# Memory heads' weighted sums with the values stationary, and the last tile's products in two halves

## The chip, the core and the metric

The kernel runs on one core of one Trainium2 chip. The metric is the device time of one execution in microseconds; for several runs the median is given. The profiled execution is one more run, with the hardware profiler's record of every instruction. In the profile PE is the tensor engine's matmul, PEld its weight load, DVE the vector engine, ACT the scalar engine, POOL the GpSimd engine and SP the engine that issues most of the transfers (DMAs).

## The reference

Two layers over 256 tokens of width 2048. Each layer projects the normed tokens to 7168 columns, runs three groups of heads on them and projects the result back:

```
h = rmsnorm(x);  proj = h @ w_in[l]              # 2048 -> 7168
y_a = short_gated_conv(a_x, a_b, a_c) * silu(a_g)
y_d = headnorm(diff_attention(q, k, v)) * silu(d_g)    # 6 heads of 128
mk, mv = keys and values of 256 memory tokens          # 4 heads of 128
p   = softmax(rmsnorm(m_q) @ mk^T / sqrt(128))
y_m = (p @ mv) * silu(m_g)                             # the memory heads
x = x + concat(y_a, y_d, y_m) @ w_out[l]
```

All of it is in float32. The changed part is `p @ mv`, its scaling by one over the softmax's sum and by the gate, and the very last tile of the last layer's output projection.

## The kernel before

Tokens lie as two tiles (t = 0, 1) of 128 rows, the width as 16 tiles k of 128. A product with a weight matrix is done by `block` (L306): 512 output columns, all k, both token tiles, with the turned tokens as the stationary side and the weights as the moving side. Float32 accuracy comes from splitting: each operand is a rounded part hi and a remainder lo, both in the type fp32r, and `products` (L298) issues three matmuls (hi hi, hi lo, lo hi). Weights come in by `load_w` (L283), two k at a time: SP loads a raw tile (L288), ACT rounds it to hi (L291), DVE subtracts to get lo (L292). There are four raw buffers and four pairs of hi and lo; a pair of buffers feeds 12 block matmuls.

Attention runs beside the blocks as generators. After each two k of a block `run_side` steps every generator that is due; a `yield n` asks to be stepped again n such steps later. Instructions marked by `keep_in_program_order` stay in the order in which they are written on their engine; the others (matmuls, weight loads) are placed by a scheduler.

Heads go in pairs, by `pair` (L501), for differential and memory heads alike. Its stages for two memory heads:

- `mem_scores` (L589): split queries and keys, six matmuls of 128x256 for each head (L604 to L606), the maximum, exp into a tile e with its sums, and r = gain / sum.
- DVE turns e in blocks of 32x32 into a sheet `sh` (L516), and `carry` (L416) brings the blocks to their places through DRAM: four DMAs out (L421), two steps later four DMAs back (L425), all on SP.
- `weighted` (L437): for each head four matmuls of 128x128 in plain float32 (L442), with the turned exp as the stationary side and the values as the moving side; the result po has queries as rows. The profile counts each plain float32 matmul as two.
- `mem_out` (L619): yn = po times r times the gate (L621), two DVE instructions for each head.
- yn is turned in blocks (L533), carried through DRAM as well, and `split_T` (L254) splits the turned result into hi and lo columns of yT, the stationary side of the output projection: ACT for hi (L258), DVE for lo (L259).

The counters `held` keep the generators from holding more than two buffers of a kind. The tiles tagged `v` and `ga` hold the differential heads' values and gate.

The output projection is four blocks of 512 columns. The products with the heads' k of the first two blocks come first, then those with the convolution's. In the last layer's last block `apart=4` puts the second token tile's products for the last four k at the very end, in `late` (L330). Then each tile's result is added to xs in halves of 256 columns (L1081), and each half is sent out (L1084), the first by SP's queue, the second by ACT's.

Of the kernel before, what the change touches and what calls it, by code (L numbers as in the profile page):

```python
# [10 lines left out]
F32 = mybir.dt.float32  # L11
F32R = mybir.dt.float32r
I32 = mybir.dt.int32
AF = mybir.ActivationFunctionType
ALU = mybir.AluOpType
# [3 lines left out]
P = 128  # L19
D_MODEL = 2048  # L20
SEQ = 256
DEPTH = 2
NT = SEQ // P
# [4 lines left out]
CG = W_CONV // P  # L28
DH = W_DIFF // P
# [3 lines left out]
NB = 512  # L33
CK = 2
PARTS = 8
B = 32
NA = P // B
PAIR_EVERY = 9
# [9 lines left out]
def encoder(ctx: ExitStack, tc: tile.TileContext, x, mem, norm_g, w_in, conv_w, conv_b,  # L48
            dq_g, dk_g, lq1, lk1, lq2, lk2, head_g, mem_norm_g, w_mem_kv, mq_g, mk_g, w_out, out):
    nc = tc.nc  # L50
# [9 lines left out]
    keep = pool("keep", 1)  # L60
    tmp = pool("tmp", 2)
    small = pool("small", 3)
    dram = pool("dram", 1, bass.MemoryType.DRAM)
    ps_acc = pool("ps_acc", 4, PSUM)
    ps_s = pool("ps_s", 2, PSUM)
    ps_t = pool("ps_t", 2, PSUM)
# [3 lines left out]
    def nm(s):  # L70
        uid[0] += 1
        return f"{s}_{uid[0]}"
# [181 lines left out]
    def split_T(dst, k, src, gain, pin=False):  # L254

        hi, lo = dst[:, 0, k, :], dst[:, 1, k, :]
        if gain is None:
            both = (nc.scalar.copy(hi, src),  # L258
                    nc.vector.tensor_tensor(lo, src, hi.bitcast(F32), ALU.subtract))  # L259
        else:  # L260
            both = (nc.scalar.activation(hi, src, AF.Copy, scale=gain),  # L261
                    nc.vector.scalar_tensor_tensor(lo, src, gain, hi.bitcast(F32), ALU.mult, ALU.subtract))
        if pin:
            for i in both:
                tc.keep_in_program_order(i)
        made.add((id(dst), k))
# [31 lines left out]
    def products(stat, acc, t, k, hi, lo, first, last, pinned=False):  # L298
        sh = stat[:, 0, k, t * P:(t + 1) * P]
        sl = stat[:, 1, k, t * P:(t + 1) * P]  # L300
        for left, right, start, stop in ((sh, hi, first, False), (sh, lo, False, False), (sl, hi, False, last)):
            i = nc.tensor.matmul(acc, left, right, start=start, stop=stop)  # L302
            if pinned:
                tc.keep_in_program_order(i)

    def block(stat, w, cols, order, steps=1, apart=0, acc=None, more=False, rows=row_tiles, ready=None):  # L306


        begun = acc is not None
        if not begun:  # L310
            acc = accumulators()
        n = len(order)

        def ends(k):
            return k == order[0] and not begun, k == order[-1] and not more

        late = []
        for c in range(0, n, CK):
            k0 = order[c]
            parts = ready(c // CK) if ready else load_w(rows(w, k0), cols)  # L320
            for j in range(CK):
                k = k0 + j
                settle(stat, k)
                for t in range(NT):
                    if t > 0 and c >= n - apart:
                        late.append((t, k, *parts[j]))
                    else:
                        products(stat, acc[t], t, k, *parts[j], *ends(k))
            run_side(steps)
        for t, k, hi, lo in late:  # L330
            products(stat, acc[t], t, k, hi, lo, *ends(k))
        return acc

    def row_stats(ss, tag):
# [81 lines left out]
    def carry(sheet, to):  # L416


        d = dram.tile([NA, B, NA, sheet.shape[-1]], F32, name=nm("d"))
        for a in range(NA):  # L420
            tc.keep_in_program_order(nc.sync.dma_start(d[:, :, a].rearrange("b c r -> c b r"), sheet[a * B:(a + 1) * B]))  # L421
        yield 2
        of = d.rearrange("b c a (n i) -> (b c) a n i", i=B)
        for a in range(NA):
            tc.keep_in_program_order(nc.sync.dma_start(to[:, :, a], of[:, a]))  # L425
# [8 lines left out]
    def strips(v):  # L434
        return v.rearrange("p (b c) -> p b c", c=B)
# [61 lines left out]
    scored = set()  # L497

    held = {"e": 0, "sh": 0, "yn": 0}

    def pair(heads, begin, end, v):  # L501

        es = []
        for h in heads:
            while held["e"] == 2:
                yield 1
            held["e"] += 1
            es.append((yield from begin(h)))
            yield 2
        yield 4  # L510
        while held["sh"] == 2:
            yield 1
        held["sh"] += 1
        sh = tmp.tile([P, NA, 2, NT * NT, B], F32, tag="sh", name=nm("sh"))
        for i, e in enumerate(es):
            tc.keep_in_program_order(nc.vector.transpose(  # L516
                sh[:, :, i], e[0].rearrange("p t (k b c) -> p b (t k) c", k=NT, b=NA)))
            held["e"] -= 1
            yield 1
        yield 4  # L520
        flat = sh.rearrange("p b h n c -> p (b h n c)")
        yield from carry(sh.rearrange("p b h n c -> p b (h n c)"), flat.rearrange("p (n a i) -> p n a i", a=NA, i=B))
        eT = flat.rearrange("p (h t k q) -> p h t k q", h=2, t=NT, k=NT)
        while held["yn"] == 2:
            yield 1
        held["yn"] += 1
        yn = tmp.tile([P, NA, 2, NT, B], F32, tag="yn", name=nm("yn"))
        for i, h in enumerate(heads):
            end[0](h, yn[:, :, i], weighted(eT, i, v, h), *es[i][1:])
            yield 2  # L530
        held["sh"] -= 1
        yield 5
        tc.keep_in_program_order(nc.vector.transpose(yn, yn))  # L533
        yield 5
        flat = yn.rearrange("p b h t c -> p (b h t c)")
        yield from carry(yn.rearrange("p b h t c -> p b (h t c)"), flat.rearrange("p (n a i) -> p n a i", a=NA, i=B))
        for i, h in enumerate(heads):
            end[1](h, flat[:, i * SEQ:(i + 1) * SEQ])
            yield 1
        held["yn"] -= 1  # L540
# [75 lines left out]
        nc.vector.tensor_tensor(r, r, st[:, HR], ALU.mult)  # L616
        return e, r

    def mem_out(h, yn, po, r, a):  # L619
        for i in range(NT):  # L620
            nc.vector.scalar_tensor_tensor(yn[:, :, i], strips(po[:, i, :]), r[:, i:i + 1],  # L621
                                           strips(a[:, i, h * P:(h + 1) * P]), ALU.mult, ALU.mult)

    def rows_T(src, k, n):

# [53 lines left out]
    def T_tile(what):  # L679
        kept.append(big.tile([P, 2, KT, SEQ], F32R, tag="T", name=nm(what)))  # L680
        return kept[-1]
# [14 lines left out]
    pin = tc.keep_in_program_order  # L696
# [48 lines left out]
    class Memory:  # L745
# [66 lines left out]
        def split(self, k, turned):  # L812
            for j, pt in enumerate(turned):
                split_T(memT, k + j, pt, None, pin=True)

    mkT, mv, stm, away = [], [], [], []
# [81 lines left out]
    while s < DEPTH * KT:  # L898
        l, k = divmod(s, KT)
# [24 lines left out]
    for l in range(DEPTH):  # L924
        st = stats_of(ssx, "st")
# [3 lines left out]


        yT = T_tile("yT")
        k2 = keep.tile([P, 2, DH - 4, SEQ], F32R, tag="bgT", name=nm("k2"))

        def x_block(cols, order=ALLK, **how):
# [2 lines left out]
        def begin_pair(n, p):  # L937
            tasks.append(later(p, max(1, start + PAIR_EVERY * n - chunk[0])))
# [4 lines left out]
        for b in order:  # L943
            if b in begun:
                acc = x_block([(C_D + b * NB, NB)], ALLK[-QT:], acc=begun[b])
            else:
                acc = x_block([(C_D + b * NB, NB)], ready=m.ready if l == 0 and b == order[0] else None)
            if b == 3:
                v = keep.tile([P, NT, W_DIFF], F32, tag="v", name=nm("v"))
                ga = keep.tile([P, NT, W_DIFF], F32, tag="ga", name=nm("ga"))  # L950
            if b == 4:
                start = chunk[0]
# [20 lines left out]
        acc = x_block([(C_M, NB)])  # L973
# [7 lines left out]
        acc = x_block([(C_M + W_MEM, NB)])  # L981
        for t in range(NT):
            silu2(mga[:, t, :], acc[t], st, t)
        def mem_done(h, y):
            assert all((l, d) in scored for d in range(DH))
            split_T(yT, CG + DH + h, y, None, pin=True)

        for n in range(MH // 2):
            begin_pair(DH // 2 + n, pair((2 * n, 2 * n + 1), lambda h: mem_scores(l, h, st),
                                         (lambda h, yn, po, r: mem_out(h, yn, po, r, mga), mem_done), mv[l]))  # L990


        bg = sheet(keep, "bgx", CG)
# [79 lines left out]
        for b in range(4):  # L1073
            final = l + 1 == DEPTH
            acc = block(yT, w_out[l], [(b * NB, NB)], convs if b < 2 else heads + convs,
                        apart=4 if final and b == 3 else 0, acc=accs[b] if b < 2 else None)
            for t in range(NT):
                n = 256 if final else NB
                for lo in range(0, NB, n):
                    xc = xs[:, t, b * NB + lo:b * NB + lo + n]  # L1080
                    nc.vector.tensor_tensor(xc, acc[t][:, lo:lo + n], xc, ALU.add)  # L1081
                    if final:
                        eng = nc.scalar if lo else nc.sync
                        eng.dma_start(out[t * P:(t + 1) * P, b * NB + lo:b * NB + lo + n], xc)  # L1084
                if not final:
                    x_square(b, t)
            if l + 1 < DEPTH:
                tasks.append(later(x_next(xT, l + 1, b), 5))
# [31 lines left out]
```

## Time and profile before

| | |
|---|---|
| median of 3 runs | 924.28 us (923.7 to 924.42) |
| profiled execution | 923.66 us, of it span 921.9 us |
| TensorE matmuls busy | 916.2 us, 99% of the span |
| VectorE, ScalarE busy | 670.0 us (73%), 498.2 us (54%) |
| TensorE clock | 1.0 of full speed over the span |
| traffic | 215.13 MB, mean 233 GB/s |

The span is the time from the first to the last record of the execution. Groups are sets of instructions of one line, engine, operation and tile: the numbers behind the bar are their busy time, the mean duration of one in ns, the idle time of the engine before them and what ended it. A matmul's record covers its way through the array, and records of successive matmuls overlap; the distance from start to start is what one costs in a stream. The chain that ended last is followed back from the last instruction, and tells on which engine the end depends.

### The profile page before, as it was taken

Reading aid. Unit: us, or ns where it says so; the run is one execution under the profiler, and the core shown is the slowest. Engines: PE = TensorE matmul, PEld = TensorE weight load, DVE = VectorE, ACT = ScalarE, POOL = GpSimd, SP = SyncE. Lnnn points to the kernel's source line nnn. Section 1 sums busy time; section 2 is a strip of 40 time slices with the busy share of each in tenths; the row PEclk is TensorE's granted clock in tenths of the full one; section 3 lists DMA queues with packets and bytes.
Section 4 is the critical chain, followed back from the end, with each engine's and each line's share of the span. In section 5 each row is a group of like instructions: output and inputs, shape, how many; then the busy total and the mean of one; then the engine's idle time right before and its main releaser. Section 6 shows DMA issues by size and latency. Waiting matters only on the chain.

```text
span 921.9 us, 12335 instructions
## 1 busy us (share of the span) xinstructions
PE 916.2 (99%) x4184; PEld 760.6 (83%) x4184; DVE 670.0 (73%) x1192; ACT 498.2 (54%) x765; POOL 36.7 (4%) x66
## 2 busy tenths in 40 slices
PE   9999999999999999999999999999999999999998
PEld 6888888888888888888888888888888888888886
DVE  5579978857798696467676757878898777458652
ACT  5667645675545554445555554568554554446431
POOL 2334010000000000000000000000000000000000
PEclk9999999999999999999999999999999999999999
DMA  8889877976669988999687766885889897979662
GB/s 289 289 244 267 272 240 223 268 212 196 182 215 246 245 246 247 229 283 259 216 265 233 246 190 219 239 231 181 242 230 227 250 232 219 265 239 256 209 221 73
DMA packets 247024, 215.13 MB, mean 233 GB/s; under 512 B 132130, under 2 KB 172912, under 8 KB 246960
## 3 DMA queue, kind: packets, MB, share of 16 engines
q1 hardware_dynamic: 242080, 208.71, 77.5%
q0 software_dynamic: 3680, 4.56, 2.1%
q10 hardware_dynamic: 1200, 1.07, 0.4%
q8 instruction: 33, 0.54, 0.2%
q14 instruction: 31, 0.25, 0.1%
HBM read 193.26 MB, written 20.97 MB: 232 GB/s over the span
## 4 chain that ended last, share of the span: by engine, by line
PE 99%; ACT 0%; DVE 0%; issue 0%; DVEq 0%
PE acc L302 94%; PE po L442 2%; PE s L550 1%; PE s L549 1%; PE pt L629 0%; PE acc L799 0%; PE s L606 0%; PE s L604 0%; PE s L605 0%; PE warm L123 0%; ACT hi L781 0%; DVE lo L782 0%; DVE xs L1081 0%; ACT memT L258 0%; DVEq L1115 0%
## 5 line engine op out<-in xcount | busy, mean ns | idle before, releaser
L302 PE MATMUL acc<-hi,xT 128*128 128x512 f32 x1792 | 559.6, 390 | 0.0
L292 DVE TENSOR_TENSOR lo<-raw,hi 128x1024 fp32r<-128x1024 f32 x280 | 342.0, 1223 | 182.5 <-ACT hi L291 176.5
L291 ACT CAST hi<-raw 128x1024 fp32r<-128x1024 f32 x280 | 294.4, 1052 | 333.1 <-PE acc L302 268.9
L302 PEld LDWEIGHTS acc<-hi,xT 128*128 128x128 f32 x1792 | 336.4, 188 | 69.0
L302 PE MATMUL acc<-lo,xT 128*128 128x512 f32 x896 | 349.0, 389 | 0.0
L302 PEld LDWEIGHTS acc<-lo,xT 128*128 128x128 f32 x896 | 168.3, 188 | 33.6
L302 PE MATMUL acc<-hi,yT 128*128 128x512 f32 x512 | 157.9, 389 | 0.0
L302 PEld LDWEIGHTS acc<-hi,yT 128*128 128x128 f32 x512 | 96.1, 188 | 19.9
L302 PE MATMUL acc<-lo,yT 128*128 128x512 f32 x256 | 99.6, 389 | 0.0
L302 PE MATMUL acc<-hi,memT 128*128 128x512 f32 x248 | 78.4, 393 | 0.0
L302 PEld LDWEIGHTS acc<-lo,yT 128*128 128x128 f32 x256 | 48.0, 188 | 10.0
L302 PEld LDWEIGHTS acc<-hi,memT 128*128 128x128 f32 x248 | 46.0, 188 | 9.5
L782 DVE SCALAR_TENSOR_TENSOR lo<-raw,cva,hi 128x1024 fp32r<-128x1024 f32 (+1 forms) x34 | 41.0, 1219 | 15.0 <-ACT hi L781 14.8
L302 PE MATMUL acc<-lo,memT 128*128 128x512 f32 x124 | 48.0, 391 | 0.3 <-DVE lo L782 0.3
L781 ACT ACTIVATE hi<-raw,cva 128x1024 fp32r<-128x1024 f32 (+1 forms) x34 | 36.6, 1099 | 10.7 <-DMA raw<-in_w_mem_kv_dram 6.4
L302 PEld LDWEIGHTS acc<-lo,memT 128*128 128x128 f32 x124 | 23.3, 188 | 5.7 <-DVE lo L782 0.9
L560 ACT ACTIVATE e<-e,mx 128x256 f32<-128x256 f32 x48 | 23.8, 499 | 1.4 <-DVE mx L556 1.3
L646 POOL DMA_DIRECT2D xt<-in_x_dram x32 | 21.5, 680 | 18.8 <-DVE rsy L186 14.2
L404 DVE STREAM_TRANSPOSE sh<-sh 128x1024 f32<-128x1024 f32 (+2 forms) x14 | 17.3, 1238 | 0.0
L554 DVE SCALAR_TENSOR_TENSOR e<-dist,s 128x512 f32<-128x512 f32 x24 | 15.7, 680 | 2.2 <-PE s L550 1.7
L261 ACT ACTIVATE xT<-xf,gx 128x256 fp32r<-128x256 f32 x32 | 14.4, 501 | 4.7 <-DVE xf L652 4.0
L1081 DVE TENSOR_TENSOR xs<-acc,xs 128x256 f32<-128x256 f32 (+1 forms) x24 | 10.9, 505 | 7.8 <-PE acc L302 7.8
(168 smaller groups left out, 598.8 us busy)
## 6 DMA issues: line engine op xcount, KB each, us to landing
raw<-in_w_in_dram SPq DMA_DIRECT2D x192, 512.0 KB, 4.3
raw<-in_w_out_dram SPq DMA_DIRECT2D x64, 512.0 KB, 4.3
raw<-in_w_in_dram SPq DMA_DIRECT2D x64, 256.0 KB, 4.4
raw<-in_w_mem_kv_dram SPq DMA_DIRECT2D x30, 512.0 KB, 6.0
d<-sh SPq DMA_DIRECT2D x80, 128.0 KB, 3.8
sh<-d SPq DMA_DIRECT2D x64, 128.0 KB, 4.0
d<-yn SPq DMA_DIRECT2D x40, 64.0 KB, 4.1
yn<-d SPq DMA_DIRECT2D x40, 64.0 KB, 3.3
```

The lines of the kernel that those rows point to most:

```text
L261: both = (nc.scalar.activation(hi, src, AF.Copy, scale=gain), nc.vector.scalar_tensor_tensor(lo, src, gain, hi.bitcast(F32), ALU.mult, ALU ...
L291: nc.scalar.copy(hi, raw)
L292: nc.vector.tensor_tensor(lo_, raw, hi.bitcast(F32), ALU.subtract)
L302: i = nc.tensor.matmul(acc, left, right, start=start, stop=stop)
L404: tc.keep_in_program_order(nc.vector.transpose(src, src))
L442: nc.tensor.matmul(po[:, t, :], eT[:, i, t, k, :], v[:, k, h * P:(h + 1) * P], start=k == 0, stop=k == NT - 1)
L554: nc.vector.scalar_tensor_tensor(e[:, c], dist, -slopes[h], s[c], ALU.mult, ALU.add)
L560: nc.scalar.activation(e[:, c, i], e[:, c, i], AF.Exp, bias=mx[:, c, i:i + 1], accum_out=sm[:, c, i:i + 1])
L646: tc.keep_in_program_order(nc.gpsimd.dma_start(st[:, n], src[n * B:(n + 1) * B].rearrange("p (b r) -> b p r", b=NA)))
L781: both = (nc.scalar.activation(hi[:, j], raw[:, j], AF.Copy, scale=g), nc.vector.scalar_tensor_tensor(lo[:, j], raw[:, j], g, hi[:, j].bit ...
L782: nc.vector.scalar_tensor_tensor(lo[:, j], raw[:, j], g, hi[:, j].bitcast(F32), ALU.mult, ALU.subtract))
L1081: nc.vector.tensor_tensor(xc, acc[t][:, lo:lo + n], xc, ALU.add)
```

## The change

For memory heads `pair`, `weighted` and `mem_out` are replaced by one generator, `mem_pair`. The stationary side of the weighted sum is now the values and the moving side the turned exp, over all 256 queries at once; both are split into hi and lo in fp32r, three matmuls for each of two tiles of memory tokens, so six of 128x256 for each head. The result has head columns as rows and queries as columns, as yT wants it, so it isn't turned any more. Instead the gate, scaled by r, is turned and carried through DRAM ahead of the sum, right behind the exp sheet, and DVE multiplies po by it. The split parts lie in tiles with the tags `v` and `ga`.

In the last block the last three of the four products set apart are issued first for columns 0 to 255, into the accumulator, and then for columns 256 to 511, into a new PSUM tile of their own. The second half is then added to xs in two steps: what the accumulator has of it, and the new tile.

```
+SPLIT = 3
...
-        for t, k, hi, lo in late:
+        whole = late[:-SPLIT] if apart else late
+        for t, k, hi, lo in whole:
             products(stat, acc[t], t, k, hi, lo, *ends(k))
+        if apart:
+            near, far = slice(0, NB // 2), slice(NB // 2, NB)
+            for t, k, hi, lo in late[-SPLIT:]:
+                products(stat, acc[t][:, near], t, k, hi[:, near], lo[:, near], *ends(k))
+            acc.append(ps_acc.tile([P, NB // 2], F32, tag="acc", name=nm("rest")))
+            for i, (t, k, hi, lo) in enumerate(late[-SPLIT:]):
+                products(stat, acc[-1], t, k, hi[:, far], lo[:, far], i == 0, i == SPLIT - 1)
         return acc
...
-    def mem_out(h, yn, po, r, a):
...
+    def mem_pair(l, n, a, st):
...
+        for i, (e, r) in enumerate(es):
+            tc.keep_in_program_order(nc.vector.transpose(
+                sh[:, :, i], e.rearrange("p t (k b c) -> p b (t k) c", k=NT, b=NA)))
+            held["e"] -= 1
+            for t in range(NT):
+                nc.vector.tensor_scalar(yn[:, :, i, t], strips(a[:, t, heads[i] * P:(heads[i] + 1) * P]),
+                                        r[:, t:t + 1], None, ALU.mult)
+            yield 1
+        tc.keep_in_program_order(nc.vector.transpose(yn, yn))
+        yield 4
+        eT = sh.rearrange("p b h n c -> p (b h n c)")
+        yT_ = yn.rearrange("p b h t c -> p (b h t c)")
+        yield from carry(sh...)
+        yield from carry(yn...)
+        if n == 0:
+            spare[l] = [keep.tile([P, 3, NB], F32R, tag=tag, name=nm(tag)) for tag in ("v", "ga")]
+        hi, lo = spare[l]
...
+        yield 1
+        for k in range(NT):
+            c = slice(k * SEQ, (k + 1) * SEQ)
+            src = mv[l][:, k, n * SEQ:(n + 1) * SEQ]
+            tc.keep_in_program_order(nc.scalar.copy(hi[:, 0, c], src))
+            tc.keep_in_program_order(nc.vector.tensor_tensor(lo[:, 0, c], src, hi[:, 0, c].bitcast(F32), ALU.subtract))
+        split(1, eT[:, 0:NB])
+        yield 1
+        split(2, eT[:, NB:2 * NB])
+        held["sh"] -= 1
+        yield 1
+        for i, h in enumerate(heads):
+            po = ps_t.tile([P, SEQ], F32, tag="t", name=nm("po"))
+            at = 0
+            for k in range(NT):
+                vh, vl = (t[:, 0, k * SEQ + i * P:k * SEQ + (i + 1) * P] for t in (hi, lo))
+                eh, el = (t[:, 1 + i].rearrange("p (t k q) -> p t k q", t=NT, k=NT)[:, :, k] for t in (hi, lo))
+                for left, right in ((vh, eh), (vh, el), (vl, eh)):
+                    nc.tensor.matmul(po, left, right, start=at == 0, stop=at == 3 * NT - 1)
+                    at += 1
+            y = yT_[:, i * SEQ:(i + 1) * SEQ]
+            nc.vector.tensor_tensor(y, po, y, ALU.mult)
+            yield 2
+            assert all((l, d) in scored for d in range(DH))
+            split_T(yTs[l], CG + DH + h, y, None, pin=True)
+        held["yn"] -= 1
...
-            begin_pair(DH // 2 + n, pair((2 * n, 2 * n + 1), lambda h: mem_scores(l, h, st),
-                                         (lambda h, yn, po, r: mem_out(h, yn, po, r, mga), mem_done), mv[l]))
+            begin_pair(DH // 2 + n, mem_pair(l, n, mga, st))
...
                     nc.vector.tensor_tensor(xc, acc[t][:, lo:lo + n], xc, ALU.add)
+                    if t == NT - 1 and lo > 0 and len(acc) > NT:
+                        nc.vector.tensor_tensor(xc, acc[NT], xc, ALU.add)
```

More of the change, by code (lines that the diff above doesn't have):

```diff
@@ L617, in mem_scores, with split @@
         return e, r
-    def mem_out(h, yn, po, r, a):
-        for i in range(NT):
-            nc.vector.scalar_tensor_tensor(yn[:, :, i], strips(po[:, i, :]), r[:, i:i + 1],
-                                           strips(a[:, i, h * P:(h + 1) * P]), ALU.mult, ALU.mult)
+    spare, yTs = {}, {}
+    def mem_pair(l, n, a, st):
+        heads = (2 * n, 2 * n + 1)
+        es = []
+        for h in heads:
+            while held["e"] == 2:
+                yield 1
+            held["e"] += 1
+            es.append((yield from mem_scores(l, h, st)))
+            yield 2
+        yield 4
+        while held["sh"] == 2 or held["yn"] == 2:
+            yield 1
+        held["sh"] += 1
+        held["yn"] += 1
+        sh = tmp.tile([P, NA, 2, NT * NT, B], F32, tag="sh", name=nm("sh"))
+        yn = tmp.tile([P, NA, 2, NT, B], F32, tag="yn", name=nm("yn"))
+        for i, (e, r) in enumerate(es):
[7 more added lines that the diff above has]
+        tc.keep_in_program_order(nc.vector.transpose(yn, yn))
+        yield 4
+        eT = sh.rearrange("p b h n c -> p (b h n c)")
+        yT_ = yn.rearrange("p b h t c -> p (b h t c)")
+        yield from carry(sh.rearrange("p b h n c -> p b (h n c)"), eT.rearrange("p (n a i) -> p n a i", a=NA, i=B))
+        yield from carry(yn.rearrange("p b h t c -> p b (h t c)"), yT_.rearrange("p (n a i) -> p n a i", a=NA, i=B))
+        if n == 0:
+            spare[l] = [keep.tile([P, 3, NB], F32R, tag=tag, name=nm(tag)) for tag in ("v", "ga")]
+        hi, lo = spare[l]
+        def split(j, src):
+            tc.keep_in_program_order(nc.scalar.copy(hi[:, j], src))
+            tc.keep_in_program_order(nc.vector.tensor_tensor(lo[:, j], src, hi[:, j].bitcast(F32), ALU.subtract))
+        yield 1
[5 more added lines that the diff above has]
+        split(1, eT[:, 0:NB])
+        yield 1
+        split(2, eT[:, NB:2 * NB])
+        held["sh"] -= 1
+        yield 1
+        for i, h in enumerate(heads):
[9 more added lines that the diff above has]
+            nc.vector.tensor_tensor(y, po, y, ALU.mult)
+            yield 2
+            assert all((l, d) in scored for d in range(DH))
+            split_T(yTs[l], CG + DH + h, y, None, pin=True)
+        held["yn"] -= 1
@@ L931, in encoder @@
         yT = T_tile("yT")
+        yTs[l] = yT
         k2 = keep.tile([P, 2, DH - 4, SEQ], F32R, tag="bgT", name=nm("k2"))
@@ L983, in encoder @@
             silu2(mga[:, t, :], acc[t], st, t)
-        def mem_done(h, y):
-            assert all((l, d) in scored for d in range(DH))
-            split_T(yT, CG + DH + h, y, None, pin=True)
         for n in range(MH // 2):
-            begin_pair(DH // 2 + n, pair((2 * n, 2 * n + 1), lambda h: mem_scores(l, h, st),
-                                         (lambda h, yn, po, r: mem_out(h, yn, po, r, mga), mem_done), mv[l]))
+            begin_pair(DH // 2 + n, mem_pair(l, n, mga, st))
         bg = sheet(keep, "bgx", CG)
```

## The prediction

> **What bounds the kernel now.** I read the page's first and fourth parts (busy time and the chain that ended last), then who waited for whom, then TensorE's instructions in order of time round one memory head and at the end.
>
> ```profile
> span 921.9 us, 12335 instructions
> PE 916.2 (99%) x4184; PEld 760.6 (83%) x4184; DVE 670.0 (73%) x1192; ACT 498.2 (54%) x765; POOL 36.7 (4%) x66
> ...
> PE 99%; ACT 0%; DVE 0%; issue 0%; DVEq 0%
> PE acc L302 94%; PE po L442 2%; PE s L550 1%; PE s L549 1%; PE pt L629 0%; PE acc L799 0%; PE s L606 0%; PE s L604 0%; PE s L605 0%; PE warm L123 0%; ACT hi L781 0%; DVE lo L782 0%; DVE xs L1081 0%; ACT memT L258 0%; DVEq L1115 0%
> ```
>
> The chain is TensorE for 99%, so a matmul that becomes shorter shortens the span by as much, as long as its operands lie ready. Whether they do is told by the waits (who, for whom, us in total, times, longest) and by three groups, the matmuls with an idle time of 0.0 and the two that make the weight parts:
>
> ```profile
> ACT hi L291 <- PE acc L302: 268.9, 176, 3.0
> DVE lo L292 <- ACT hi L291: 176.5, 175, 4.9
> ...
> ACT hi L291 <- DMA raw<-in_w_in_dram: 24.7, 12, 5.1
> ```
>
> ```profile
> L302 PE MATMUL acc<-hi,xT 128*128 128x512 f32 x1792 | 559.6, 390 | 0.0
> L292 DVE TENSOR_TENSOR lo<-raw,hi 128x1024 fp32r<-128x1024 f32 x280 | 342.0, 1223 | 182.5 <-ACT hi L291 176.5
> L291 ACT CAST hi<-raw 128x1024 fp32r<-128x1024 f32 x280 | 294.4, 1052 | 333.1 <-PE acc L302 268.9
> ```
>
> ScalarE, which rounds the weights to hi, mostly waits for TensorE to free a buffer: the weights are ahead by all four buffer pairs. Each pair feeds 12 matmuls. When TensorE frees one, 3 pairs (36 matmuls) are still ahead, and its refill takes 1.05 + 1.22 = 2.3 us.
>
> **The change on TensorE.** First the rows of one old memory head (start, duration, instruction), then of one scores step of a memory head, which issues six fp32r matmuls of 256 columns each with its own weight load, as the new weighted sum does.
>
> ```profile
> 793.25 0.40 PE L302 MATMUL acc<-hi,xT 128*128 128x512 f32 x1
> 793.48 1.06 PE L442 MATMUL po<-mv,sh 128*128 128x128 f32 x8
> 794.29 0.47 PE L302 MATMUL acc<-hi,xT 128*128 128x512 f32 x1
> 794.61 0.39 PE L302 MATMUL acc<-lo,xT 128*128 128x512 f32 x1
> ```
>
> ```profile
> 752.30 0.39 PE L302 MATMUL acc<-lo,xT 128*128 128x512 f32 x1
> 752.53 0.40 PE L302 MATMUL acc<-hi,xT 128*128 128x512 f32 x1
> 752.76 0.28 PE L604 MATMUL s<-parts 128*128 128x256 f32 x1
> 752.88 0.28 PE L605 MATMUL s<-parts 128*128 128x256 f32 x1
> ...
> 753.36 0.28 PE L606 MATMUL s<-parts 128*128 128x256 f32 x1
> 753.48 0.39 PE L302 MATMUL acc<-hi,xT 128*128 128x512 f32 x1
> 753.71 0.40 PE L302 MATMUL acc<-lo,xT 128*128 128x512 f32 x1
> ```
>
> A block matmul takes 0.227 us from start to start (752.30 to 752.53). From the last one before the head to the second one after it are 794.61 - 793.25 = 1.36 us; without the head it would be 2 x 0.227 = 0.454. So an old head costs **0.906 us**: eight fp32 passes at about 0.112 and a slow restart. The same bracket round the scores is 753.71 - 752.53 = 1.18, less 0.454: six matmuls cost **0.726 us**, 0.120 each. Eight heads in two layers: 8 x (0.906 - 0.726) = **1.44 us less**. The new moving operand is read in two runs of 128, a form that no row shows; it is bounded by 0.12 (the scores) and by the weight load's duration, 0.19 (a rival below). I take 0.12, the row with the same columns, type and loads.
>
> **The end.** The last products and what follows them:
>
> ```profile
> 917.54 0.39 PE L302 MATMUL acc<-hi,yT 128*128 128x512 f32 x1
> 917.96 0.76 DVE L1081 TENSOR_TENSOR xs<-acc,xs 128x256 f32<-128x256 f32 x2 [1.96 <-PE acc L302]
> 918.42 0.33 SPq L1084 DMA_DIRECT2D out_dram<-xs  x1
> 918.75 0.34 ACTq L1084 DMA_DIRECT2D out_dram<-xs  x1
> ```
>
> Nine 512-column matmuls become 18 of 256. First start to last end was 8 x 0.227 + 0.39 = 2.21 us and becomes 17 x 0.12 + 0.28 = 2.32: 0.11 more. From the last matmul's end (917.93) to the last issue (918.75) are 0.82 us with two adds. Now the near half's add and its DMA, and the first add of the far half, run beside the nine far matmuls (9 x 0.12 = 1.08 us against 0.76 for two adds); one add of about 0.42 is left, with the same 0.03 on either side: 0.48, 0.34 less. If that cover were gone, the third add would cost the 0.34 back. The DMA left over is as large as before and goes alone. Together **0.23 us less**.
>
> **Work put beside TensorE.** Rows for the new instructions and their room:
>
> ```profile
> L621 DVE SCALAR_TENSOR_TENSOR yn<-po,mr,mga 128x128 f32<-128x128 f32 x16 | 4.8, 340 | 0.8 <-PE po L442 0.8
> L475 DVE TENSOR_TENSOR yT<-sh,yT 64x512 fp32r<-64x512 f32 x4 | 2.7, 686 | 0.1
> L259 DVE TENSOR_TENSOR yT<-yn,yT 128x256 fp32r<-128x256 f32 x8 | 3.3, 410 | 0.0
> L474 ACT CAST yT<-sh 64x512 fp32r<-64x512 f32 x4 | 2.5, 617 | 0.0
> L258 ACT CAST yT<-yn 128x256 fp32r<-128x256 f32 x8 | 3.2, 402 | 0.1
> ```
>
> ```profile
> 350.00:370.00 20.00, 20.00 (x97) 16.78 (x97) 15.47 (x20) 8.84 (x11) 0.00 (x0) 1.00 0.79 247
> 370.00:390.00 20.00, 20.00 (x94) 16.68 (x93) 8.50 (x9) 8.16 (x9) 0.00 (x0) 1.00 1.07 239
> ...
> 760.00:780.00 20.00, 20.00 (x98) 16.78 (x97) 15.47 (x20) 8.64 (x11) 0.00 (x0) 1.00 0.76 227
> 780.00:800.00 20.00, 20.00 (x95) 16.67 (x94) 9.55 (x10) 8.62 (x9) 0.00 (x0) 1.00 1.11 247
> ```
>
> (Columns of the second: PE, PEld, DVE, ACT and POOL busy in each 20 us, clock, DMA share, GB/s.) For each pair of heads DVE gets two subtractions of 128x512 (0.69 each), two of 128x256 for the values and two products with po (0.41 each): 1.37 + 0.82 + 0.82 = 3.0 us. The four scalings by gate (0.34 at most) only replace L621's four, and the transposes stay as many. ACT gets 2 x 0.62 + 2 x 0.40 = 2.0 us. In the order of the changed program the splits come one or two weight pairs after the gated sheet's long transpose (L404), at about 366 and 778 us; the second pair of each layer falls into 390 to 410 and 800 to 820. DVE then has 18.5 busy of 20 us in the fullest stretch: it may fall behind for a moment, by 1 to 2 us, and lives on the lead over TensorE: 36 x 0.227 = 8.2 us less the 2.3, some 5.9 us (an estimate from the rows above). So these cost nothing; what would cost is a lead of zero.
>
> **The queues.** Sheet and gate are carried through DRAM before the sum, in one go on SP:
>
> ```profile
> raw<-in_w_in_dram SPq DMA_DIRECT2D x192, 512.0 KB, 4.3
> ...
> d<-sh SPq DMA_DIRECT2D x80, 128.0 KB, 3.8
> sh<-d SPq DMA_DIRECT2D x64, 128.0 KB, 4.0
> d<-yn SPq DMA_DIRECT2D x40, 64.0 KB, 4.1
> yn<-d SPq DMA_DIRECT2D x40, 64.0 KB, 3.3
> ```
>
> The number and sizes of these transfers do not change; the sheet's and the gate's ways now follow each other. Where the way back is issued one weight pair (12 x 0.227 = 2.7 us) behind the way out, SP stands for 4.1 - 2.7 = 1.4 us, with the weight loads behind it. Those are issued when a raw buffer frees, four pairs (10.9 us) before ACT needs them, and take 4.3: 6.6 us of slack, and the 5.9 behind it. POOL's queue has nothing here. VectorE's product waits for po, then for the gate's way back, with the next weights' lo behind it; the gate's DMAs are issued over 10 us earlier. The old yn was turned and carried after po, with two five-step pauses; that goes, so yT's last four columns come earlier relative to po. The second pair's scores move 36 matmuls later, on TensorE at the same cost. The buffers of v and ga that hold the parts were last read for the differential heads, some 100 matmuls before; the end's third accumulator takes a PSUM buffer that the block before has long left.
>
> **Sum.** 1.44 + 0.23 = 1.67 us. The profiled run took 923.66 with a span of 921.9, 1.76 outside it; its span would be 920.2 and it 922.0. It lies 0.62 under the median of 924.28, against which I forecast **922.6 us** (0.18% less). A measurement of this kernel can tell about 0.2%, 1.85 us, from no change; the forecast lies just inside.
>
> **Rivals.**
> *The saving is handed back* (weights, not TensorE, set the pace, so the change brings less than it says): only the 0.23 is left, 924.05. For it: 12 waits for raw weights, 24.7 us. Against: 268.9 us of waiting for TensorE. Chance 0.05.
> *The lead runs out* (slower): in the first pair of each layer SP stands with its two returns and raw weights come late while DVE is at 18.5 of 20. It decides once SP stands 12.5 us (6.6 + 5.9); each us beyond is one lost. With 2 us lost in each layer: 922.6 + 4 = 926.6. For it: the longest wait for raw weights, 5.1. Against: even that is under half of 12.5. Chance 0.07.
> *The load is not hidden* (slower): if a 256-column matmul costs its weight load, 0.19, a head costs 6 x 0.19 = 1.14, 0.23 more than the old: +1.9; the end 18 x 0.19 - 9 x 0.227 - 0.34 = +1.0: 927.2. Against: the scores' 0.12 with loads. Chance 0.03. [...]
> *Shorter still*: a step of 0.227 / 2 = 0.113 without the scores' overhead: 48 x 0.007 + 18 x 0.007 = 0.46 more, 922.1. Chance 0.05. [...]
>
> **How the numbers follow.** The forecast's case has 0.80. Its own spread, 0.4 us by the shown runs (923.7 to 924.42), puts near half of it past the 0.2% bound: 0.39 of the 0.80. With *shorter still*, faster is 0.44; same is 0.41 + 0.05 = 0.46; slower 0.10. The range, 921.8 to 924.2, takes in *shorter still* and *handed back* with the runs' spread, and leaves out the slower cases and some tails.
>
> **What would show it.** Right: po's group reads 48 fp32r matmuls of 128x256, a block matmul follows each six at 0.12, one add stands behind the last matmul, and TensorE has no new idle. Wrong: an idle of L302 behind lo or raw between 340 and 420 or 750 and 840 us; po 0.19 apart; two adds after the last product.

## The result and the profile after

| | before | after |
|---|---|---|
| median of 6 runs each | 923.77 us (923.28 to 924.42) | 927.02 us (925.93 to 928.07) |
| profiled execution, of it span | 923.66, 921.9 us | 926.78, 925.0 us |

The changed kernel takes 1.0034 of the time of the one before (95% interval 1.0024 to 1.0044): 3.25 us slower where 1.67 us less was forecast, and outside the range of 921.8 to 924.2.

The page of the changed kernel: the first part, the chain of work that ended last by engine and by line, and the group of block matmuls.

```profile
span 925.0 us, 12351 instructions
PE 917.3 (99%) x4177; PEld 761.3 (82%) x4177; DVE 680.4 (74%) x1217; ACT 505.7 (55%) x781; POOL 36.6 (4%) x66
...
PE 94%; SPq 3%; DMA 1%; DVE 1%; issue 0%; ACT 0%; ACTq 0%; DVEq 0%
PE acc L303 89%; DMA raw<-in_w_in_dram 1%; SPq L434 1%; PE po L451 1%; SPq L430 1%; PE s L559 1%; PE s L558 1%; DVE lo L293 0%; PE acc L870 0%; PE po L686 0%; PE pt L700 0%; SPq L289 0%; PE warm L124 0%; ACT hi L292 0%; PE s L615 0%
...
L303 PE MATMUL acc<-hi,xT 128*128 128x512 f32 x1792 | 560.0, 391 | 1.9 <-ACT hi L292 1.9
```

TensorE's busy share still reads 99%, but the chain is no longer TensorE alone: SP's issues of the carries (L430 out, L434 back) and the landing of raw weights are on it. The matmul group, which had no idle time, has 1.9 us behind hi. Whom ScalarE waits for, when it makes hi, has moved from TensorE to the raw weights (us in total, times, longest):

```profile
ACT hi L292 <- PE acc L303: 230.5, 156, 3.0
...
ACT hi L292 <- DMA raw<-in_w_in_dram: 56.4, 31, 7.0
```

Before, the waits for raw weights were 24.7 us, 12 times, at most 5.1. The place is seen in TensorE's instructions in order of time, and in the busy times round it (PE, PEld, DVE, ACT, POOL, then the clock, the DMA share and GB/s):

```profile
394.05 0.39 PE L303 MATMUL acc<-hi,xT 128*128 128x512 f32 x1
396.37 0.50 PE L303 MATMUL acc<-hi,xT 128*128 128x512 f32 x1 [1.93 <-ACT hi L292]
397.63 0.56 PE L303 MATMUL acc<-lo,xT 128*128 128x512 f32 x1 [0.76 <-DVE lo L293]
397.99 1.05 PE L303 MATMUL acc<-hi,xT 128*128 128x512 f32 x2
398.84 0.63 PE L303 MATMUL acc<-lo,xT 128*128 128x512 f32 x1
399.27 1.05 PE L303 MATMUL acc<-hi,xT 128*128 128x512 f32 x2
400.12 0.63 PE L303 MATMUL acc<-lo,xT 128*128 128x512 f32 x1
400.55 1.00 PE L303 MATMUL acc<-hi,xT 128*128 128x512 f32 x2
401.38 0.39 PE L303 MATMUL acc<-lo,xT 128*128 128x512 f32 x1
```

```profile
396.50:402.00 5.50, 4.74 (x13) 3.52 (x14) 4.80 (x6) 4.06 (x6) 0.00 (x0) 0.69 1.04 253
402.00:408.00 6.00, 6.00 (x28) 4.95 (x28) 5.29 (x6) 3.37 (x5) 0.00 (x0) 1.00 1.05 358
```

From the start at 394.05 to the one at 401.38 are 11 steps in 7.33 us, where 11 x 0.227 = 2.50 would do: 4.83 us lost. Two pauses make 3.12 of it: 396.37 - 394.05 - 0.227 = 2.09 for hi, and 397.63 - 396.37 - 0.227 = 1.03 for the lo that is subtracted after it. The other 1.7 us are a slower clock: after the pauses three matmuls take 400.12 - 398.84 = 1.28 us, 0.427 each, and the granted clock is 0.69 over 5.5 us; in the 6 us behind it is 1.00 again. The trace's clock records put it at 0.50 for 3.41 us from 397.94 on.

Why were the weights late? SP's instructions in order of time, first of the kernel before and then of the changed one. Each row is a group of DMAs issued one behind the other; L288 and L289 are the raw weights; most of these loads bring the weights of a whole pair of k, but the last two at 384.19 and the last four at 390.85 are halves of a pair's weights.

```profile
367.44 3.57 SPq L425 DMA_DIRECT2D sh<-d  x4
371.11 1.26 SPq L288 DMA_DIRECT2D raw<-in_w_in_dram  x2
372.46 6.81 SPq L425 DMA_DIRECT2D bgT<-d  x4
379.38 1.75 SPq L288 DMA_DIRECT2D raw<-in_w_in_dram  x2
381.17 2.92 SPq L421 DMA_DIRECT2D d<-yn  x4
384.19 1.43 SPq L288 DMA_DIRECT2D raw<-in_w_in_dram  x3
```

```profile
345.58 0.39 SPq L289 DMA_DIRECT2D raw<-in_w_in_dram  x1
346.08 2.14 SPq L434 DMA_DIRECT2D yn<-d  x4
348.38 3.44 SPq L434 DMA_DIRECT2D sh<-d  x4
351.87 3.82 SPq L430 DMA_DIRECT2D d<-yn  x4
355.78 1.43 SPq L289 DMA_DIRECT2D raw<-in_w_in_dram  x3
...
373.12 2.42 SPq L430 DMA_DIRECT2D d<-sh  x4
375.65 5.25 SPq L434 DMA_DIRECT2D bgT<-d  x4
381.00 2.70 SPq L289 DMA_DIRECT2D raw<-in_w_in_dram  x2
383.79 4.67 SPq L434 DMA_DIRECT2D sh<-d  x4
388.51 2.25 SPq L430 DMA_DIRECT2D d<-yn  x4
390.85 2.46 SPq L289 DMA_DIRECT2D raw<-in_w_in_dram  x5
```

A group of four carries holds SP for 2 to 7 us in the issuing instructions themselves, and the loads behind it in the queue go out only after it. Before, loads stand between every two of the groups shown: seven from 371.11 to 385.62. In the changed kernel the sheet's way back and the gate's way out are neighbours (348.38 and 351.87 for the first pair of heads, 383.79 and 388.51 for the second). Twice that shows: from 345.97 to 355.78 SP issues 12 carries and no weights (9.8 us), and from 373.12 to 390.85, 17.7 us, it issues two loads, while TensorE uses up one per 2.72. The lead (from the end of a pair's lo to its first matmul, worked out from the records) is 5.6 us for the last pair loaded before the first of these; for the next, used at 363 us, it is 0.9, recovers to 5.5 at 386, and is below zero at 396: the pair that TensorE waits for was loaded by the issue at 390.85. Its raw buffer had been free since 378.15, when the lo that read it ended, so the load went out 12.7 us later (5.6 for the same pair in the kernel before); it landed 4.3 us after its issue, where 4.4 is the median, so the transfer itself was not slow. In the kernel before the lead is nowhere under 2.2 us once the first pairs are through (up to 110 us it is as low as 1.3 in both kernels), and it is 4.7 for that pair.

### The profile page after: what moved, and what is told of

Read it like the earlier page. It is cut to its first block, busy times and chain, and to the rows that moved or that the text cites. A ratio compares the mean times of both kernels' runs of the same rounds, so it can differ in the third digit from the quotient of the medians.

```text
span 925.0 us, 12351 instructions
## 1 busy us (share of the span) xinstructions
PE 917.3 (99%) x4177; PEld 761.3 (82%) x4177; DVE 680.4 (74%) x1217; ACT 505.7 (55%) x781; POOL 36.6 (4%) x66
## 2 busy tenths in 40 slices
DMA packets 247023, 215.11 MB, mean 233 GB/s; under 512 B 132130, under 2 KB 172912, under 8 KB 246960
## 4 chain that ended last, share of the span: by engine, by line
PE 94%; SPq 3%; DMA 1%; DVE 1%; issue 0%; ACT 0%; ACTq 0%; DVEq 0%
PE acc L303 89%; DMA raw<-in_w_in_dram 1%; SPq L434 1%; PE po L451 1%; SPq L430 1%; PE s L559 1%; PE s L558 1%; DVE lo L293 0%; PE acc L870 0%; PE po L686 0%; PE pt L700 0%; SPq L289 0%; PE warm L124 0%; ACT hi L292 0%; PE s L615 0%
## 5 line engine op out<-in xcount | busy, mean ns | idle before, releaser
L303 PE MATMUL acc<-lo,yT 128*128 128x512 f32 (+1 forms) x256 | 99.3, 388 | 0.0
L262 ACT ACTIVATE xT<-xf,gx 128x256 fp32r<-128x256 f32 x32 | 14.4, 501 | 4.8 <-DVE xf L723 4.0
L723 DVE STREAM_TRANSPOSE xf<-xt 128x1024 f32<-128x1024 f32 x8 | 16.1, 2012 | 0.0
```

The source lines that it names most:

```text
L723: tc.keep_in_program_order(nc.vector.transpose(whole.rearrange("p j (n i) -> p j n i", i=B), st.rearrange("p n (c j) -> p j n c", j=QT)))
```

## The experiments

Theory Q: SP's queue. The carries that were moved together keep SP from issuing weights. Rival V: VectorE's and ScalarE's added work makes hi and lo late. Rival T: the added or moved transfers slow the weights on the DMA engines. Ratios are to the kernel before, run on the same chip, with the 95% interval.

### One part at a time

The end alone, put into the kernel before:

```
+SPLIT = 3
-        for t, k, hi, lo in late:
+        whole = late[:-SPLIT] if apart else late
...
```

> Only the last tile's end is changed; the memory heads are as before. Queue theory (the change loses time because the carries of sheet and gate stand ahead of weight loads in SP's queue in layer 0): nothing of that is here, so 0.2 us less than before (0.34 saved on the adds, 0.11 to 0.12 paid on TensorE), no idle of TensorE after the start. If the end itself were a loss (weight loads not hidden at 256 columns): about 1 us more than before.

Measured: 924.13 us, 0.9997 (0.9988 to 1.0005), which can't tell 0.23 us from nothing. The trace can: from the last matmul's end to the end of the span were 921.9 - 917.93 = 3.97 us, and in the changed kernel they are 925.0 - 921.42 = 3.58; in this run 3.60. The rows of the changed kernel:

```profile
920.38 0.76 DVE L1148 TENSOR_TENSOR xs<-acc,xs 128x256 f32<-128x256 f32 x2 [1.00 <-PE acc L303]
921.14 0.28 PE L303 MATMUL rest<-hi,yT 128*128 128x256 f32 x1
921.46 0.42 DVE L1150 TENSOR_TENSOR xs<-rest,xs 128x256 f32<-128x256 f32 x1 [0.32 <-PE rest L303]
```

Two adds end beside the far matmuls, one of 0.42 is left.

The sums alone, the changed kernel with the old end:

```
-        whole = late[:-SPLIT] if apart else late
-        for t, k, hi, lo in whole:
+        for t, k, hi, lo in late:
...
```

> Only the memory heads are changed; the end is as before. Queue theory: some 3.4 us slower than before, as TensorE waits for weight parts near 396 us in layer 0 and then runs some 2 us at a lower granted clock, against 1.4 us saved on the sums. If the end were the loss: 1.4 us faster than before.

Measured: 928.18 us, 1.0042 (1.0024 to 1.006). The loss belongs to the sums. In the profiled run TensorE pauses at 396.4 (1.02 and 0.76 us idle) and, shorter, at 813 and 819, with no fall of the clock (1.0 over the span).

The new sums in layer 1 only (with the new end):

```
-            begin_pair(DH // 2 + n, mem_pair(l, n, mga, st))
+            begin_pair(DH // 2 + n, mem_pair(l, n, mga, st) if l == 1 else
+                       pair((2 * n, 2 * n + 1), lambda h: mem_scores(l, h, st),
+                            (lambda h, yn, po, r: mem_out(h, yn, po, r, mga), mem_done), mv[l]))
```

> The new sums in layer 1 alone, the old ones in layer 0, the new end. Queue theory with the loss in layer 0: 0.7 us saved on four heads and 0.2 at the end, 0.9 us faster than before. In the trace of the changed kernel layer 1's weight parts came as late as TensorE wanted them (a lead of zero at one place), and two other traces show waits of 1 to 2 us there: if these are the rule, as slow as before or 1 us slower.

Measured: 923.69 us, 0.9997 (0.9989 to 1.0006). The pause near 396 is gone, two of 0.34 and 0.35 us idle (0.5 each from start to start) stand at 810 and 816. So layer 0's stretch makes most of the loss. The expected gain of 0.9 us (a ratio of 0.9990) lies at the edge of the interval and is not shown; in the profiled run the two pauses cost 1.0 us, about as much.

### The queue

Both carries of the memory pairs from POOL's queue, all else as changed:

```
-    def carry(sheet, to):
+    def carry(sheet, to, queue=nc.sync):
...
-        yield from carry(sh...)
-        yield from carry(yn...)
+        yield from carry(sh..., nc.gpsimd)
+        yield from carry(yn..., nc.gpsimd)
```

> The changed kernel with the memory heads' carries issued from POOL's queue in place of SP's: same transfers, same bytes, same VectorE work. Queue theory: weight loads go out on time, no idle of TensorE after the start, 1.4 to 1.7 us faster than before (922.1 where before is 923.8). VectorE theory (3.0 us more per pair make lo late): still slower than before by 2 to 3 us. Transfer theory (the DMA engines are full, whoever issues): still slower by 2 to 3 us, weight loads take longer to land.

Measured: 922.65 us, 0.9984 (0.9976 to 0.9993), 1.65 us under the 924.3 beside it, about the sum that was forecast. The busy times of one stretch, of this run and then of the changed kernel:

```profile
340.00:404.00 64.00, 64.00 (x295) 53.38 (x294) 45.21 (x64) 33.44 (x48) 21.77 (x32) 1.00 1.00 279
```

```profile
340.00:404.00 64.00, 61.31 (x273) 50.34 (x273) 40.71 (x60) 30.58 (x46) 0.00 (x0) 0.97 0.96 244
```

TensorE is busy for all 64 us although VectorE and ScalarE did more in them, against V. The waits for raw weights fall to 29.4 us. The loads issued between 340 and 402 us even take longer to land than in the changed kernel (median 5.8 and at most 10.9 us, there 4.7 and 5.7), and TensorE doesn't wait: they go out early enough, which speaks against T. But POOL's queue moves the same bytes in fewer packets (219,887 for the whole kernel against 247,023), so a part could be T.

Only the gate's carry from POOL's queue (the second of the two lines), and in a later run only the sheet's (the first):

> The changed kernel with only the gate's carry (8 of 16 DMAs a pair) issued from POOL; the exp sheet's stays in SP's queue, next to bgT's as before. Queue theory: SP issues 8 transfers less between weight loads, about 4 to 6 us of its time a pair; TensorE waits little or not, 922.2 to 923.2 where before is 923.8 to 924.3. If it took the whole of the carries to fill SP: still 1 us or more slower than before.

> The changed kernel with the sheet's two ways on POOL's queue and the gate's on SP, the counterpart of the run that moved the gate alone (still 0.18% slower). Theory (SP's issue time; the sheet's transfers with the beta and gate ones beside them are what empties the lead): no pause of TensorE near 390 to 400 us, about as with both on POOL, 922.2 to 923.4. Rival (either carry left on SP is enough): a pause of 1 to 3 us stays, 925 to 927.

Measured: the gate alone 926.11 us, 1.0018 (1.001 to 1.0027); the sheet alone 924.97 us, 1.0012 (1.0002 to 1.0021). Both times the theory's expectation missed: each carry that stays on SP is enough for a pause. With the gate moved away it is 0.82 and 0.76 us idle at 391, and from 373.48 to 391.53 SP still issues twelve carries with two loads among them. With the sheet moved away 0.71 us idle are left at 390, in a profiled run (923.43 us) that was the fastest of ten. In these two runs Q is not the whole account. The loads that came late went out 7.2 and 6.6 us after their buffers had come free, but they also took 7.7 and 7.5 us to land, 3 us over the median. Why is open, so T may have a part here.

The same transfers on SP, but three steps between the sheet's carry and the gate's:

```
         yield from carry(sh...)
+        yield 3
         yield from carry(yn...)
```

> The changed kernel with three more steps between the exp sheet's way back and the gate's way out, all still in SP's queue: as many transfers, as much VectorE work, other neighbours in the queue. Queue theory: weight loads go out between the groups, the wait near 396 us goes or falls below 1 us, 922.2 to 923.5. If the amount of transfers or VectorE's work is the cause: as slow as the changed kernel, 3 us over before.

Measured: 923.13 us, 0.9987 (0.9978 to 0.9996). Packets, bytes and the work of VectorE are those of the changed kernel; only the order in SP's queue differs. The rows of SP to compare with the changed kernel's:

```profile
382.08 6.91 SPq L434 DMA_DIRECT2D sh<-d  x4
389.09 2.60 SPq L289 DMA_DIRECT2D raw<-in_w_in_dram  x5
391.74 1.98 SPq L430 DMA_DIRECT2D d<-yn  x4
```

Five loads (one whole and four halves) go out at 389.09, ahead of the gate's way out, where the changed kernel has them at 390.85 behind it. Of the 3.1 us of pauses 0.18 is left. The margin is that thin: the lead of the same pair is -0.35 here, -1.20 in the changed kernel.

### The dose, without the change

The kernel before, with one more carry (eight DMAs of 64 KB, the gate into an unused tile) for each pair of memory heads on SP; nothing is added on TensorE, ScalarE or VectorE:

```
...
+        if more is not None:
+            extra = tmp.tile([P, NB], F32, tag="eT", name=nm("extra"), bufs=1)
+            yield from carry(more..., extra...)
...
```

> The kernel before, untouched but for one more carry on SP for each pair of memory heads: four DMAs of 64 KB out and four back, of the gate into a tile that nothing reads, right behind the exp sheet's way back. No instruction more on VectorE, ScalarE or TensorE; the old sums stand two steps later. Queue theory: weight loads come late in layer 0 where these stand beside bgT's carry, TensorE waits, 1 to 5 us slower than before. VectorE theory: as before, within 0.5 us.

And the same extra carry from POOL's queue (`carry(more..., extra..., nc.gpsimd)`):

> The dose of the run before it (one more carry of eight 64 KB transfers per pair of memory heads, put into the old kernel, 0.59% slower on SP's queue) is issued from POOL's queue; the bytes stay, the issue time leaves SP. Theory (SP's issue time between two weight loads): no idle time of TensorE at 390 to 398 us, the kernel within 0.1% of the kernel before, 923.5 to 925. Rival (the extra traffic itself, half a megabyte each way per pair, delays the weights): the pause at 393 us stays, 927 or more.

Measured: on SP 930.26 us, 1.0059 (1.0046 to 1.0072); on POOL 924.96 us, 1.0007 (0.9998 to 1.0017). The dose on SP makes the whole picture in the old kernel, pause and slow clock (granted 0.79 from 390 to 398 us, 1.00 in the 6 us after):

```profile
392.89 0.50 PE L302 MATMUL acc<-hi,xT 128*128 128x512 f32 x1 [2.63 <-ACT hi L291]
394.15 0.77 PE L302 MATMUL acc<-lo,xT 128*128 128x512 f32 x1 [0.76 <-DVE lo L292]
...
395.57 0.63 PE L302 MATMUL acc<-lo,xT 128*128 128x512 f32 x1
```

On SP the load that TensorE waits for went out 14.4 us after its buffer had come free and landed 4.6 us later. The same bytes (256 KB each way for a pair; the second expectation's half a megabyte is twice too much) from another queue leave TensorE without a pause there. V is excluded as a necessary cause, T too as far as bytes go; the packets were not held constant (10,752 more than before on SP, 1,024 on POOL). The other queue was worth 5.3 us here (930.26 - 924.96), the packets' unknown part included.

### Moves that cost elsewhere

The split's subtractions of sheet and values on POOL instead of VectorE:

```
-            tc.keep_in_program_order(nc.vector.tensor_tensor(lo[:, j], src, ...))
+            tc.keep_in_program_order(nc.gpsimd.tensor_tensor(lo[:, j], src, ...))
```

> The changed kernel with the four subtractions for lo of sheet and values done on POOL in place of VectorE: 2.2 us less for VectorE per pair, SP's queue written in the same way. Queue theory: still slower than before by 2.5 to 3.5 us, the same wait near 396 us. VectorE theory: 1.4 to 1.7 us faster than before.

Measured: 930.0 us, 1.0066 (1.0053 to 1.0079). From 360 to 404 us VectorE is busy for 24.16 us, in the changed kernel for 27.76, and the pauses stay and are more (0.67 and 0.76 at 390, 1.60 and 0.76 at 398; the wait for raw weights is 63.1 us in all). The late loads went out 9.4 and 12.0 us after their buffers had come free. V falls; why they became more was not followed up.

Both carries from ScalarE's queue (`nc.scalar` in place of `nc.gpsimd`), where they have the same packets as on SP (247,023 in all):

> The changed kernel with the memory heads' carries issued from ACT's queue: the same hardware transfers in the same small packets as on SP (on POOL's queue they went in fewer, larger packets), only out of the way of the weight loads. Queue theory: SP issues the weight loads without groups between them, no wait for raw weights beyond those of the kernel before; what ScalarE's own standing for the issues costs hi (16 issues of 0.4 to 1 us a pair) comes out of the lead, 922.3 to 924. Packet theory (the many packets of 128 bytes hold up the weight loads wherever they are issued): weight loads still late near 396 us, 926 to 927.

Measured: 932.87 us, 1.0099 (1.0083 to 1.0116). The wait for raw weights falls to 28.2 us, as Q says. But now ScalarE, which makes hi, is the one that stands: from 805.80 to 813.46 it issues DMAs, and hi stands behind them.

```profile
805.80 4.88 ACTq L434 DMA_DIRECT2D sh<-d  x3
810.72 2.74 ACTq L430 DMA_DIRECT2D d<-yn  x4
813.58 1.99 ACT L292 CAST hi<-raw 128x1024 fp32r<-128x1024 f32 x2 [7.39 <-DMA d<-yn]
```

TensorE is idle for 3.44 us up to 814.7, and in the same way for 1.44 us up to 397.6. The expected time was missed: the expectation counted ScalarE's issues (0.4 to 1 us each) and let the lead pay for them, but seven in a row took 7.7 us here, more than the lead of 5.9, with hi behind them.

The weight loads from POOL's queue, the carries on SP:

```
-            nc.sync.dma_start(raw[:, :, at:at + n], rows[:, :, lo:lo + n])
+            nc.gpsimd.dma_start(raw[:, :, at:at + n], rows[:, :, lo:lo + n])
```

> The changed kernel with the weight loads of all projection blocks issued from POOL's queue, and all carries left on SP as they are: the small packets of the carries stay. Queue theory: no weight load stands behind a carry, TensorE does not wait near 396 us; 1.4 to 1.7 us faster than before, about 922.5, unless POOL's own loads at about 90 us come late. Packet theory (the carries' packets of 128 bytes hold up the weights' transfers): TensorE still waits 2 us or more between 380 and 402 us, 926 to 927.

Measured: 932.44 us, 1.0083 (1.0066 to 1.01), far from the 922.5 expected; the profiled run took 937.42. In the disputed stretch Q holds: TensorE is busy for all of it, with the small-packet carries still on SP.

```profile
340.00:404.00 64.00, 64.00 (x295) 53.40 (x294) 49.00 (x92) 33.87 (x53) 17.85 (x26) 1.00 0.90 248
```

The time goes elsewhere, to the differential heads, whose sums wait for a sheet:

```profile
262.92 1.55 PE L451 MATMUL po<-v,sh 128*128 128x128 f32 x8 [3.00 <-DMA sh<-d]
330.74 2.05 PE L451 MATMUL po<-v,sh 128*128 128x128 f32 x8 [5.59 <-DMA sh<-d]
```

A sheet's way back lands 6.3 us after its issue here (median), 4.3 in the changed kernel. Why it lands later was not settled.

## Why the prediction was wrong

- **The queues: the step that failed.** It priced SP's standing by the wait for a landing, 4.1 - 2.7 = 1.4 us, and the issuing itself at nothing. But the rows of the carries before hold SP for 0.5 to 1.7 us per DMA, and in the changed kernel the three groups from 346.08 on, one behind the other, held SP for 9.6 us by issuing. The wait that was priced did not grow: SP waited for the landings of these ways out for 19.2 us in the whole run before and for 17.6 after. The sentence that the number and sizes of the transfers do not change was true and beside the point: what changed is how many of them lie between two weight loads. The diff and the order of the changed program show that; SP's rows of before (groups of four at 2 to 7 us) have the price. The prediction neither counts nor shows them.
- **The slack.** 5.9 us of lead is right for the steady state (5.6 worked out), and 6.6 of landing slack was taken on top of it as if all of it were free in every stretch. One standing of 9.8 us already took 4.7 us of lead; what emptied it was a second and third standing, 7.9 and 7.2 us with two loads between, before the lead had been filled again. One long standing alone did no harm: before, SP issues 16 carries and no weights from 701.33 to 710.71, 9.4 us, and TensorE doesn't wait.
- **The rival.** *The lead runs out* named the mechanism and nearly the time: 926.6 against 927.02. Its place was one pair off: the first pair's carries only took the lead down to 0.9, the second pair's emptied it, in the profiled run in one layer only. Its condition was wrong in form: one standing of 12.5 us instead of the loads issued over a stretch against the 2.72 us at which they are used. With that condition its chance of 0.07 would have had to be far larger. It priced a lost microsecond as one; the run showed 3.1 of pauses and 1.7 more of clock.
- **TensorE's saving: right.** In the run with the carries on POOL's queue a new head stands like this:

```profile
376.78 0.39 PE L303 MATMUL acc<-hi,xT 128*128 128x512 f32 x1
377.00 0.28 PE L686 MATMUL po<-v 128*128 128x256 f32 x1
...
377.94 0.40 PE L303 MATMUL acc<-lo,xT 128*128 128x512 f32 x1
```

  The bracket is 377.94 - 376.78 - 0.454 = 0.706 us, forecast 0.726: 0.20 saved per head, 1.6 in all instead of 1.44. *The load is not hidden* falls: the matmuls follow at 0.12, the moving side in two runs of 128 included.
- **The end: right.** 0.39 less behind the last matmul, where 0.34 was forecast, and the 0.11 on TensorE ahead of it.
- **Work beside TensorE: right.** The new rows measure 0.67, 0.41 and 0.42 us on VectorE, 3.0 per pair, and 0.62 and 0.40 on ScalarE, 2.0 per pair, as forecast. From 360 to 404 us, which takes in the splits of two pairs, VectorE is busy for 2.8 us more than before (27.76 against 24.92) and ScalarE for 4.5 (22.15 against 17.65); that the 2.8 is near the 3.0 of one pair is chance, as one lo of 1.2 us fewer falls into the stretch and old work goes. With the carries on POOL this costs nothing: TensorE is busy for all 64 us from 340 to 404.
- ***The saving is handed back*** falls: where SP does not stand, the run takes 0.9984, the whole forecast. ***Shorter still*** asked for a step of 0.113, so 0.684 us per head; the 0.706 lies about halfway to it, and the times (interval from 0.9976 on) can't tell the two apart.

The balance of the profiled runs: 4.8 lost near 396, 1.6 and 0.3 (0.39 less the 0.11) gained, so +2.9 of the +3.1 in the span. The rest is not placed; the first ten microseconds alone differ by up to about 1 us between runs.

## What to carry to other kernels

On a queue that also feeds the bound engine, count the issue time of every DMA, by its row, and hold the loads issued over a stretch against the rate at which they are used; a group moved next to another adds no bytes, but it can keep the loads back for longer than the lead lasts, as here, where one went out 12.7 us after its buffer had come free. Here three steps between two carries, or an idle queue for both, turned +0.34% into about -0.15%, a version faster than either kernel. Before moving a carry to an engine, look at what that engine makes for the bound one, and price a pause of the tensor engine with the slower clock that can follow it, here 1.7 us on top of 3.1.

## What the runs showed of the hardware

- A pause could cost more than its length: in the changed kernel 1.93 and 0.76 us of idle time were followed by 0.427 us per matmul, with the granted clock at 0.50 for 3.41 us. The length of a pause alone does not decide it. After 1.02 and 0.76 us (the sums alone) and even after 1.60 and 0.76 us (the subtractions on POOL) the clock stayed at 1.00, but with the gate alone moved 0.82 and 0.76 us were followed by a slower one: 0.42 us per matmul from 393.93 on, and a mean clock of 0.998 over the run. What else decides was not measured. The rows of that last run:

```profile
390.92 0.50 PE L303 MATMUL acc<-hi,xT 128*128 128x512 f32 x1 [0.82 <-ACT hi L292]
392.18 0.51 PE L303 MATMUL acc<-lo,xT 128*128 128x512 f32 x1 [0.76 <-DVE lo L293]
...
393.93 0.63 PE L303 MATMUL acc<-lo,xT 128*128 128x512 f32 x1
394.35 1.05 PE L303 MATMUL acc<-hi,xT 128*128 128x512 f32 x2
```

- The same form of DMA held SP for very different times: four of `sh<-d` took 3.44, 4.67 and 6.91 us in the rows above, four of `bgT<-d` 5.25 and 6.81. Whether this is a backlog in front of the DMA engines or something else stays open.
- POOL's queue moved the same carries in fewer packets: 27,136 fewer for the 32 DMAs of the sheets and the 32 of the gates. Since the spaced version, with all the small packets, gains nearly as much as POOL's queue (0.9987 against 0.9984), the packets are at most a small part of the effect; they were not isolated. POOL's issues were steady, 0.55 us for each way out and 0.75 and 0.88 for the ways back, where single carries on SP took up to 3.5 in the changed kernel.
